# Splitting the eight PSUM banks two to six, not three to five, in the middle stage of a hybrid transformer layer

## Chip, cores and metric

The kernel runs on one core of a Trainium2 chip. The metric is the device time of one execution in microseconds (us). The core has five engines that run side by side: PE (matrix products, with weight loads listed apart as PEld), DVE, ACT and POOL (elementwise work) and SP (which issues transfers). Matrix products land in PSUM, which has eight banks of 128 x 512 fp32 values; another engine must read a result out of its bank ("evict" it) before the bank can hold the next one.

## The reference

One inference step of one layer, in fp32, on 256 prompt tokens and 8 decode tokens (one new token for each of 8 sequences). Model width 2048, FFN width 5504.

```python
x = x + 0.5 * swiglu(rmsnorm(x, n1), f1g, f1u, f1d)      # first FFN
h = rmsnorm(x, nm)
proj = h @ w_in                                           # 2048 x 4864
# columns of proj: q (1024), k, v (256 each), and the RWKV columns
o_att  = attend(q, k, v, sinks)        # window 128, 16 q heads, 4 kv heads
o_rwkv, shift, S = rwkv_time_mix(proj[..., ATT_COLS:], shift0, wkv0, ...)
x = x + concat([o_att, o_rwkv]) @ w_out                   # 2048 x 2048
x = x + 0.5 * swiglu(rmsnorm(x, n2), f2g, f2u, f2d)      # second FFN
y = rmsnorm(x, final_norm)
```

The RWKV-7 part mixes each token with its predecessor, and then runs, for each of 16 heads, a recurrence over a 64 x 64 state: `S = S*exp(logw) + (S @ -kk) * (kk*a) + v * k`, output `S @ r`. Outputs are y for both kinds of tokens, the new key and value caches, the RWKV states and the last projected columns.

## The kernel before

**Layout and precision.** Activations lie with features on the 128 partitions and the T = 264 tokens (256 + 8) along the free axis, so x is 16 tiles of 128 x 264. Each fp32 product is made of three: weights and activations are split into a rounded part (`hi`) and a rest (`lo`), and `gemm` (L143) issues hi·hi, hi·lo and lo·hi for each 128 x 128 weight block. The weights stream from memory in chunks of four blocks: `chunk` (L125) issues the transfer on SP into one of seven `raw` buffers, ACT casts `hi` (in the profile L136), and DVE subtracts for `lo` (L58), seven buffers each.

**Stages.** The first FFN (0 to about 706 us of the trace), the middle stage (to about 1133 us), and the second FFN. In each FFN the 43 blocks of the FFN width are handled in six parts; a part computes gate and up products, then 16 down products of eight or seven blocks (24 or 21 matmuls), each of which DVE adds to the residual from its bank (L297, recorded in the profile as L61). In the last part each such tile is also split and squared for the next norm (`nxt`), a square on ACT and a sum on POOL.

**The middle stage** (`mixing_body`) computes 38 input products of 48 matmuls each (`win(t)`, L411): two for the low-rank RWKV columns, 24 for r, k, v of eight head pairs, four for attention's k and v, eight for q. Its large products are evicted on DVE with high priority. The small work is written as generators: `prep` (a head pair's decay, keys and inner products), `chain` (a batch of two pairs: a triangular inverse by forward substitution on DVE with tiles `X`, `Xt`, `st`, then matrix products and the state passing), `attend` (one q tile of attention: scores, softmax, transposes, values), `kvtask`, `dec_load` and `dec_attend` (decode attention). After each weight chunk `tick` advances every live generator by one step, so small products are strewn among the large ones. Last comes the output projection, in three passes over 4, 6 and 6 of the 16 `mixed` tiles (`PASS`); each pass makes 16 products of 12 or 18 matmuls, adds them to the residual `xr`, and starts when the tiles it needs are mixed and split (`split`, L936; the cast is L939).

**Banks.** One pool `pp` holds all PSUM: tag `acc`, NACC = 3 banks, for large products, tag `m`, NM = 5 banks, for small ones and the first part of each FFN. `acc()` and `mp()` hand out the next bank of a kind, and whoever gets it waits until its last content has been read. In the middle stage a bank of kind `m` serves everything from the inner products of `prep` to transposes.

**Order.** A list scheduler with a cost model (not the order of the code alone) sets the order of instructions on each engine; within an engine they run in this order. Priorities, `keep_in_program_order` and `issue_after` bind it at places. In the profile all elementwise calls through helpers carry the helper's line: `tt` L58, `stt` L61, `act` L68, `mm` L74.

Of the kernel before, what the change touches and what calls it, by code (L numbers as in the profile page):

```python
# [7 lines left out]
F32 = mybir.dt.float32  # L8
# [5 lines left out]
P = 128  # L14
# [11 lines left out]
PARTS = [8, 7, 7, 7, 7, 7]  # L26
BATCH = [2, 2, 2, 2]
CH, NRAW, NHL = 4, 7, 7
NACC, NM = 3, 5
NS, NO, NY, NH, NT, NLD = 38, 8, 8, 40, 18, 6  # L30
NWARM = 7
NGM, NKR, NUV, NTT, NBT = 10, 5, 3, 2, 5
# [15 lines left out]
def body(tc, I, O):  # L48
# [4 lines left out]
    def uid(s):  # L53
        cnt[0] += 1
        return f"{s}{cnt[0]}"

    def tt(e, out, a, b, op):
        return e.tensor_tensor(out=out, in0=a, in1=b, op=op)  # L58
# [8 lines left out]
    def act(out, in_, f, **k):  # L67
        return A.activation(out=out, in_=in_, func=f, **k)  # L68
# [4 lines left out]
    def mm(out, lhsT, rhs, start=True, stop=True, **k):  # L73
        TE.matmul(out, lhsT, rhs, start=start, stop=stop, **k)  # L74
# [17 lines left out]
    def drain(only, hold=()):  # L92
        while any(g in only for g in tasks):
            tick(hold)
# [9 lines left out]
    with ExitStack() as ctx:  # L104
        cp = ctx.enter_context(tc.tile_pool(name="cp", bufs=1))
        sp = ctx.enter_context(tc.tile_pool(name="sp", bufs=1))
        wp = ctx.enter_context(tc.tile_pool(name="wp", bufs=1))
        pp = ctx.enter_context(tc.tile_pool(name="pp", bufs=1, space=bass.MemoryType.PSUM))
        dp = ctx.enter_context(tc.tile_pool(name="dp", bufs=1, space=bass.MemoryType.DRAM))
        cur = [None]  # L110

        def slot(shape=(P, T), dt=F32, tag="s"):
            return sp.tile(list(shape), dt, tag=tag, bufs={"s": NS, "o": NO, "y": NY}[tag], name=uid(tag))
# [3 lines left out]
            return pool.tile(list(shape), dt, tag="t", bufs=n, name=uid("t"))  # L117

        def acc():
            return pp.tile([P, 512], F32, tag="acc", bufs=NACC, name=uid("acc"))  # L120

        def mp():
            return pp.tile([P, 512], F32, tag="m", bufs=NM, name=uid("m"))

        def chunk(src, n, ahead=True):  # L125
            w = n * P
# [33 lines left out]
        ones = cp.tile([P, P], F32, name="ones")  # L160
# [3 lines left out]
        G.memset(eps[:, 1:2], 64e-5)  # L164
        act(eps[:, 0:1], eps[:, 0:1], AF.Copy)

        warm = mp()
        for _ in range(NWARM):
            mm(warm[:, :P], ones, ones)

        def vc(i):
            return vec[:, i:i + 1]
# [129 lines left out]
        def first_ffn(n2):  # L302
            xr = []

            def load(k0):
                n1.split(xr[k0], k0 > 1, e=None if k0 else V)

            def nxt(o):
                n2.split(xr[o])
                n2.square(xr[o])  # L310
                A.dma_start(xsp[o], xr[o])

            with tc.tile_pool(name="f1", bufs=1) as fp:
                cur[0] = (fp, NH)
                keep = tc.keep_in_program_order

                def weights(i):
                    raw = wp.tile([P, CH * P], F32, tag="raw", bufs=NRAW, name=uid("raw"))
                    keep(SP.dma_start(raw[:, :2 * P], I["gu1"][i // 2, i % 2][:, :2 * P]))
                    pre.append(raw)  # L320

                def inputs(n):
                    xg = fp.tile([P, n, T], F32, name=f"xg{len(xr)}")
                    k = KD + len(xr) * T
                    keep(SP.dma_start(xg.rearrange("p k t -> p (k t)"), I["xT"][:, k:k + n * T]))
                    xr.extend(xg[:, j] for j in range(n))

                def begin(k0, i):
                    n = {(2, 0): 2, (2, 2): 2, (4, 1): 2, (4, 3): 2, (8, 1): 2, (8, 3): 2}.get((k0, i))
                    if n:  # L330
                        inputs(n)

                x0 = fp.tile([P, T + KD], F32, name="x0")
                keep(SP.dma_start(x0, I["xT"][:, :T + KD]))
                n1 = Norm(VG1, gain=x0[:, T:])
                xr.append(x0[:, :T])
                for i, n in enumerate((1, 0, 0, 0, 0, 2)):
                    weights(i)
                    if n:
                        inputs(n)  # L340
                ffn(n1, xr, I["gu1"], I["dn1"], nxt, load, begin)
# [30 lines left out]
        def mixing(n2, n3, XD):  # L372
            with tc.tile_pool(name="mx", bufs=1) as mx:
                cur[0] = (mx, NT)
                return mixing_body(mx, n2, n3, XD)

        def mixing_body(mx, n2, n3, XD):
# [33 lines left out]
            def win(t):  # L411
                ps = acc()
                gemm(ps, I["win"][t], n2.xs, tick)
                if not have[0]:
                    n2.rstd(rs)
                    have[0] = True
                return ps
# [478 lines left out]
            for kind, i in SEQ:  # L896
# [10 lines left out]
                elif kind == "kv":  # L907
                    w, p = i // 2, i % 2
                    ps = win(LKV + i)
# [6 lines left out]
                else:  # L916
                    ps = win(LKV + 4 + i)
# [14 lines left out]
            xr = [slot() for _ in range(KD)]  # L932
# [3 lines left out]
            def split(i):  # L936
                hi, lo = slot(dt=F32R), slot(dt=F32R)
                m = pairs(mixed[i])
                A.copy(halves(hi), m)  # L939
                tt(V, halves(lo), m, halves(hi).bitcast(F32), ALU.subtract)  # L940
                mixed[i] = (hi, lo)

            def need(ks):
                return [bat[k // 2] for k in ks if k < 8] + [g for k in ks if k > 7 for g in att[k - 8]]

            k0 = 0
            for pi, ks in enumerate(PASS):
                now = need(ks)
                drain(now, [g for g in tasks if g not in now])
                with tc.high_priority():  # L950
                    for k in ks:
                        split(k)
                for o in range(KD):
                    ps = acc()
                    gemm(ps, I["wout"][o, :, k0 * P:(k0 + len(ks)) * P], [mixed[k] for k in ks], tick)
                    with tc.high_priority():
                        tt(V, xr[o], ps[:, :T], xr[o], ALU.add)
                    if pi == len(PASS) - 1 and o < CH:
                        n3.split(xr[o], tag="y")
                for k in ks:  # L960
                    mixed[k] = None
                k0 += len(ks)
            return xr

        def second_ffn(n3, xr, XD):
            fin = Norm(VGF, 3)

            def load(k):
                if k >= CH:
                    n3.split(xr[k], True, "o" if k in NSO else "s")  # L970

            with tc.tile_pool(name="f2", bufs=1) as fp:
                cur[0] = (fp, NH)
                ys = [fp.tile([P, 4, T], F32, tag="y", bufs=4, name=uid("y")) for _ in range(4)]
                rt = fp.tile([88, 8], F32, name="rt")

                def nxt(o):
                    fin.square(xr[o])
                    if o == 0:
                        act(rt[:, 7:8], fin.sums[0][0][0:88, 0:1], AF.Sqrt)  # L980
                    act(ys[o // 4][:, o % 4], xr[o], AF.Copy, scale=vc(VGF + o))

                side = dec_state(fp, XD)
                ffn(n3, xr, I["gu2"], I["dn2"], nxt, load, False, side)
                assert next(side, side) is side
                p = fin.sums[0]
                sm, rp, rq, hot = (mp() for _ in range(4))
                for i, q in enumerate(p):
                    for j in range(3):
                        mm(sm[0:88, j:j + 1], q[:, j * 88:j * 88 + 88], ones[:, 0:1], i + j == 0, i > 0,  # L990
                           skip_group_check=True)
                for _ in range(4):
                    mm(hot[:, :P], ones, p[1][:, :P])
                act(rt[:, 0:3], sm[0:88, 0:3], AF.Sqrt, scale=1.0 / D, bias=eps[0:88, 0:1])
                V.reciprocal(rt[:, 0:3], rt[:, 0:3])
                for r in (rp, rq):
                    for j in range(3):
                        mm(r[:, j * 88:j * 88 + 88], bc(rt[:, j:j + 1], (88, P)), C[0:88, CID:CID + 88])
                rs = fp.tile([P, T], F32, name="rs")
                A.copy(rs, rq[:, :T])  # L1000
                for i, (o, n) in enumerate(((0, 1), (1, 1), (2, 2), (12, 1), (4, 4), (13, 1), (8, 2), (14, 1), (10, 2), (15, 1))):
                    y = ys[o // 4][:, o % 4:o % 4 + n]
                    e, r = (V, rp[:, :T]) if o < 12 else (G, rs)
                    tt(e, y, y, bc(r.unsqueeze(1), (P, n, T)), ALU.mult)
                    (SP, A)[i % 2].dma_start(O["yT"][:, o:o + n, :], y)

        xsp = [dp.tile([P, T], F32, tag=f"xsp{o}", name=f"xsp{o}") for o in range(KD)]
        n2, n3 = Norm(VGM), Norm(VG2)
        first_ffn(n2)
        with tc.tile_pool(name="dx", bufs=1) as dx:  # L1010
            XD = dx.tile([P, 8, NPAIR, NB], F32, name="XD")
            second_ffn(n3, mixing(n2, n3, XD), XD)


OUTS = dict(yT=(P, KD, T), kp=(2, P, P), vp=(2, P, P), ks=(NB, P, 256), vs=(NB, P, 256),
# [99 lines left out]
```

## Time and profile before

| | us |
|---|---|
| median of three runs (lowest, highest) | 1848.77 (1846.81, 1850.28) |
| profiled execution | 1846.21 |
| its span | 1844.4 |
| PE busy in the span | 1821.4 |
| middle stage, 706 to 1133 us: length | 427.0 |
| middle stage: PE busy | 415.9 |
| middle stage: DVE busy | 349.3 |
| middle stage: ACT busy | 307.3 |

In rows of single instructions the first number is the start in us, the second the duration, then engine, line, operation, output and inputs, and in square brackets the time that the engine stood idle just before and what ended it. Durations of matmuls overlap, since they are pipelined; the step from one start to the next is what each costs. In rows of stretches the clock is the share of full speed that PE was granted. Tile names are without numbers: `acc` and `m` are banks, `s`, `t`, `o`, `y` activation tiles, `xg` the residual of the first FFN.

### The profile page before, as it was taken

The page shows a single profiled execution, that of the slowest core. Times are in us where ns is not written, and L with a number is a line of the kernel's source. Part 1 is how long each engine was busy: PE and PEld are TensorE (multiplying, and loading weights), DVE is VectorE, ACT ScalarE, POOL GpSimd, SP SyncE. Part 2 cuts the span into 40 slices and gives each one's busy share as a digit, 9 for nine tenths or more (in the row PEclk, how much of TensorE's full clock was granted, in tenths as well). Part 3 has the DMA queues.
Part 4 walks back from the last instruction along what each step waited for, and adds up shares of the span by engine and source line. Part 5 has one row for each costly group of instructions (what it writes and reads, how often), then busy time and mean ns, then how long its engine had stood idle before and what let it go on. Part 6 is the DMA issues. An engine that isn't in the chain of part 4 may idle for free.

```text
span 1844.4 us, 46192 instructions
## 1 busy us (share of the span) xinstructions
PE 1821.4 (99%) x17212; PEld 1792.4 (97%) x17212; DVE 1311.4 (71%) x2613; ACT 1068.6 (58%) x2134; POOL 258.4 (14%) x389
## 2 busy tenths in 40 slices
PE   9999999999999999999998999999999999999998
PEld 9999999999999999998987899999999999999997
DVE  6966665656656577799888677876766676667765
ACT  6645555455554557777767766654545555455555
POOL 0401101010010122122111200220101001010012
PEclk9999999999999999999999999999999999999999
DMA  8666666666666677555666446666666666666664
GB/s 270 191 202 213 196 210 205 201 199 188 204 190 201 196 201 244 174 169 146 174 174 183 143 127 220 185 201 189 203 207 208 193 211 203 203 208 193 216 189 136
DMA packets 226465, 358.25 MB, mean 194 GB/s; under 512 B 38440, under 2 KB 82112, under 8 KB 226240
## 3 DMA queue, kind: packets, MB, share of 16 engines
q1 hardware_dynamic: 220352, 349.20, 62.9%
q10 hardware_dynamic: 5888, 6.11, 1.1%
q8 instruction: 135, 2.21, 0.5%
q14 instruction: 90, 0.74, 0.1%
HBM read 347.06 MB, written 10.22 MB: 194 GB/s over the span
## 4 chain that ended last, share of the span: by engine, by line
PE 91%; DVE 3%; DMA 3%; issue 1%; ACT 1%; POOL 0%; SPq 0%; POOLq 0%; ACTq 0%; DVEq 0%
PE acc L74 84%; PE m L74 6%; DVE lo L58 1%; DMA raw<-in_gu 1%; DMA raw<-in_win 0%; DVE Xt L58 0%; DVE st L58 0%; DMA X<-sa 0%; ACT hi L136 0%; DMA sa<-gm 0%; DMA out_vp<-s 0%; DVE t L61 0%; DMA s<-xsp 0%; DVE t L459 0%; DMA ld<-in_bias 0%
## 5 line engine op out<-in xcount | busy, mean ns | idle before, releaser
L58 DVE TENSOR_TENSOR lo<-raw,hi 128x512 fp32r<-128x512 f32 (+2 forms) x1312 | 876.5, 673 | 443.9 <-ACT hi L136 417.2
L136 ACT CAST hi<-raw 128x512 fp32r<-128x512 f32 (+2 forms) x1312 | 774.9, 596 | 665.0 <-PE acc L74 438.8
L74 PE MATMUL acc<-s,hi 128*128 128x264 f32 x5940 | 1030.6, 278 | 2.7 <-ACT s L939 1.2
L74 PEld LDWEIGHTS acc<-s,hi 128*128 128x128 f32 x5940 | 899.3, 189 | 9.4 <-ACT hi L136 2.2
L74 PE MATMUL acc<-s,lo 128*128 128x264 f32 x2970 | 824.2, 278 | 0.0
L74 PEld LDWEIGHTS acc<-s,lo 128*128 128x128 f32 x2970 | 561.8, 189 | 2.3 <-issue 0.9
L74 PE MATMUL acc<-t,hi 128*128 128x264 f32 x2752 | 465.0, 276 | 0.0
L74 PEld LDWEIGHTS acc<-t,hi 128*128 128x128 f32 x2752 | 414.9, 189 | 0.0
L74 PE MATMUL acc<-t,lo 128*128 128x264 f32 x1376 | 379.2, 276 | 0.0
L58 POOL TENSOR_TENSOR t<-t,t 128x264 f32<-128x264 f32 (+1 forms) x148 | 145.3, 981 | 1063.6 <-ACT hi L136 986.0
L74 PEld LDWEIGHTS acc<-t,lo 128*128 128x128 f32 x1376 | 260.1, 189 | 0.0
L74 PE MATMUL acc<-y,hi 128*128 128x264 f32 x648 | 113.8, 277 | 0.0
L74 PEld LDWEIGHTS acc<-y,hi 128*128 128x128 f32 x648 | 97.8, 189 | 0.2
L74 PE MATMUL acc<-y,lo 128*128 128x264 f32 x324 | 89.4, 276 | 0.0
L58 DVE TENSOR_TENSOR t<-acc,t 128x264 f32<-128x264 f32 x156 | 67.2, 431 | 20.6 <-PE acc L74 12.0
L58 POOL TENSOR_TENSOR o<-o,o 128x264 f32<-128x264 f32 x43 | 35.7, 829 | 195.8 <-ACT o L68 189.0
L74 PEld LDWEIGHTS acc<-y,lo 128*128 128x128 f32 x324 | 61.2, 189 | 0.0
L74 PE MATMUL acc<-o,hi 128*128 128x264 f32 x324 | 58.8, 276 | 0.0
L74 PEld LDWEIGHTS acc<-o,hi 128*128 128x128 f32 x324 | 48.8, 189 | 0.0
L61 DVE SCALAR_TENSOR_TENSOR s<-acc,s 128x264 f32<-128x264 f32 x96 | 40.9, 430 | 8.8 <-PE acc L74 6.3
L289 ACT CAST t<-t 128x264 fp32r<-128x264 f32 x86 | 38.3, 445 | 13.6 <-POOL t L58 8.1
L74 PE MATMUL m<-s,hi 128*128 128x264 f32 x260 | 44.8, 277 | 0.6 <-ACT hi L136 0.6
(246 smaller groups left out, 1266.5 us busy)
## 6 DMA issues: line engine op xcount, KB each, us to landing
raw<-in_gu SPq DMA_DIRECT2D x680, 256.0 KB, 3.4
raw<-in_dn SPq DMA_DIRECT2D x224, 256.0 KB, 3.0
raw<-in_win SPq DMA_DIRECT2D x152, 256.0 KB, 3.7
raw<-in_dn SPq DMA_DIRECT2D x160, 192.0 KB, 2.7
raw<-in_wout SPq DMA_DIRECT2D x48, 256.0 KB, 3.3
raw<-in_wout SPq DMA_DIRECT2D x32, 128.0 KB, 2.8
s<-xsp SPq DMA_DIRECT2D x16, 132.0 KB, 3.5
raw<-in_gu SPq DMA_DIRECT2D x16, 128.0 KB, 3.9
```

The lines of the kernel that those rows point to most:

```text
L58: return e.tensor_tensor(out=out, in0=a, in1=b, op=op)
L61: return V.scalar_tensor_tensor(out=out, in0=a, scalar=s, in1=b, op0=op0, op1=op1)
L74: TE.matmul(out, lhsT, rhs, start=start, stop=stop, **k)
L136: A.copy(hi[:, :w], raw[:, :w])
L289: A.copy(halves(hi), pairs(u))
```

## The change

The single pool becomes three that follow each other: `pa` for the warm-up products and the first FFN, `pb` for the middle stage, `pc` for the second FFN. The first and third have three `acc` and five `m` banks as before, the middle one two and six (`NPB` = 2). In the output projection odd products take a bank of kind `m`, even ones of kind `acc`.

```diff
-NACC, NM = 3, 5
+NACC, NM, NPB = 3, 5, 2
...
-        pp = ctx.enter_context(tc.tile_pool(name="pp", bufs=1, space=bass.MemoryType.PSUM))
...
+        @contextmanager
+        def banks_of(name, *n):
+            with tc.tile_pool(name=name, bufs=1, space=bass.MemoryType.PSUM) as pool:
+                bank[0] = (pool, *n)
+                yield
...
         def acc():
-            return pp.tile([P, 512], F32, tag="acc", bufs=NACC, name=uid("acc"))
+            pool, n, _ = bank[0]
+            return pool.tile([P, 512], F32, tag="acc", bufs=n, name=uid("acc"))
...
         def mp():
-            return pp.tile([P, 512], F32, tag="m", bufs=NM, name=uid("m"))
+            pool, _, n = bank[0]
+            return pool.tile([P, 512], F32, tag="m", bufs=n, name=uid("m"))
...
-        warm = mp()
-        for _ in range(NWARM):
-            mm(warm[:, :P], ones, ones)
+        def warm():
+            w = mp()
+            for _ in range(NWARM):
+                mm(w[:, :P], ones, ones)
...
-                    ps = acc()
+                    ps = mp() if o % 2 else acc()
                     gemm(ps, I["wout"][o, :, k0 * P:(k0 + len(ks)) * P], [mixed[k] for k in ks], tick)
...
-        first_ffn(n2)
+        with banks_of("pa", NACC, NM):
+            warm()
+            first_ffn(n2)
         with tc.tile_pool(name="dx", bufs=1) as dx:
             XD = dx.tile([P, 8, NPAIR, NB], F32, name="XD")
-            second_ffn(n3, mixing(n2, n3, XD), XD)
+            with banks_of("pb", NPB, NACC + NM - NPB):
+                xr = mixing(n2, n3, XD)
+            with banks_of("pc", NACC, NM):
+                second_ffn(n3, xr, XD)
```

Each engine gets the same instructions, but for two ACT table loads fewer; the order differs from somewhat behind the start of the middle stage to its end, and is the same in both FFNs. At the borders of the pools the first product that takes a bank of the new pool waits until the old pool's last contents have been read: the first projection product for DVE's eviction of the last down product (before, for that of two products earlier), and the first gate product of the second FFN for the eviction of the last output product.

DVE, in the middle stage: the steps `st` and `Xt` are the forward substitution of the last batch, `kr<-m` and `N<-m` are evictions of small products of the batch before it. Before:

```order
L58 TENSOR_TENSOR Xt_14789<-Xt_14789,st_15492 128x5x11
L58 TENSOR_TENSOR st_15543<-X_14788,Xt_14789 128x60
L58 TENSOR_TENSOR Xt_14789<-Xt_14789,st_15543 128x6x10
L58 TENSOR_TENSOR st_15546<-X_14788,Xt_14789 128x54
L58 TENSOR_TENSOR Xt_14789<-Xt_14789,st_15546 128x6x9
L58 TENSOR_TENSOR kr_12776<-m_15223,kr_12776 128x192
L58 TENSOR_TENSOR kr_13282<-m_15223,kr_13282 128x192
L58 TENSOR_TENSOR st_15597<-X_14788,Xt_14789 128x48
L58 TENSOR_TENSOR Xt_14789<-Xt_14789,st_15597 128x6x8
L58 TENSOR_TENSOR st_15600<-X_14788,Xt_14789 128x42
L58 TENSOR_TENSOR N_15161<-m_15252,wc 128x512
```

The same place of the changed kernel:

```order
L58 TENSOR_TENSOR Xt_14793<-Xt_14793,st_15496 128x5x11
L58 TENSOR_TENSOR st_15547<-X_14792,Xt_14793 128x60
L58 TENSOR_TENSOR kr_12780<-m_15227,kr_12780 128x192
L58 TENSOR_TENSOR kr_13286<-m_15227,kr_13286 128x192
L58 TENSOR_TENSOR Xt_14793<-Xt_14793,st_15547 128x6x10
L58 TENSOR_TENSOR st_15550<-X_14792,Xt_14793 128x54
L58 TENSOR_TENSOR Xt_14793<-Xt_14793,st_15550 128x6x9
L58 TENSOR_TENSOR N_15165<-m_15256,wc 128x512
```

The two `kr` evictions moved three substitution steps earlier, and `N` three steps as well.

PE, in attention: the four products into one bank (`m_15904` before, `m_15908` now) are the values product of one q tile, each of them behind a transposed softmax tile `t`; `acc` rows are matmuls of large products. Before:

```order
L74 MATMUL m_15851<-uv_15730,bk_15732 32x128 x8
L74 MATMUL m_15851<-s_14402,bk_15732 32x1 x8
L74 MATMUL m_15904<-t_15745,s_14845 64x256
L74 MATMUL acc_16188<-s_10600,lo_16334 128x264
L74 MATMUL m_15904<-t_15809,s_14845 64x256
L74 MATMUL m_15904<-t_15746,s_14845 64x128
L74 MATMUL acc_16421<-s_16405,hi_16423 128x264
L74 MATMUL acc_16489<-s_16405,hi_16491 128x264
L74 MATMUL acc_16604<-s_16405,hi_16606 128x264
L74 MATMUL m_15904<-t_15810,s_14845 64x128
```

The same place of the changed kernel:

```order
L74 MATMUL m_15855<-uv_15734,bk_15736 32x128 x8
L74 MATMUL m_15855<-s_14406,bk_15736 32x1 x8
L74 MATMUL m_15908<-t_15749,s_14849 64x256
L74 MATMUL acc_16053<-s_9998,lo_16056 128x264
L74 MATMUL acc_16053<-s_10041,hi_16055 128x264
L74 MATMUL acc_16053<-s_10042,hi_16055 128x264
L74 MATMUL acc_16053<-s_10041,lo_16056 128x264
L74 MATMUL acc_16053<-s_10084,hi_16055 128x264
L74 MATMUL acc_16053<-s_10085,hi_16055 128x264
L74 MATMUL m_15908<-t_15813,s_14849 64x256
L74 MATMUL m_15908<-t_15750,s_14849 64x128
```

Before, one matmul of the last projection product stands between the first two values products, and three matmuls of three begun output products follow; now six matmuls of a projection product stand there, and the output projection begins later.

More of the change, by code (lines that the diff above doesn't have):

```diff
@@ L1 @@
 import math
-from contextlib import ExitStack, nullcontext
+from contextlib import ExitStack, contextmanager, nullcontext
 import numpy as np
@@ L107, in body @@
         wp = ctx.enter_context(tc.tile_pool(name="wp", bufs=1))
-        pp = ctx.enter_context(tc.tile_pool(name="pp", bufs=1, space=bass.MemoryType.PSUM))
         dp = ctx.enter_context(tc.tile_pool(name="dp", bufs=1, space=bass.MemoryType.DRAM))
-        cur = [None]
+        cur, bank = [None], [None]
+        @contextmanager
[3 more added lines that the diff above has]
+                yield
         def slot(shape=(P, T), dt=F32, tag="s"):
```

## The prediction

> **What bounds the kernel now.** I read the page's shares first, then the span cut at the two stage borders, then what TensorE (PE) waits for in the middle stage, then single stretches in time order.
>
> ```profile
> PE 1821.4 (99%) x17212; PEld 1792.4 (97%) x17212; DVE 1311.4 (71%) x2613; ACT 1068.6 (58%) x2134; POOL 258.4 (14%) x389
> 0.00:706.00 706.00, 703.13 (x6214) 701.46 (x6215) 470.08 (x792) 383.77 (x695) 91.93 (x101) 1.00 0.68 205
> 706.00:1133.00 427.00, 415.88 (x4753) 389.34 (x4752) 349.28 (x978) 307.32 (x762) 75.97 (x190) 1.00 0.59 171
> 1133.00:1844.40 711.40, 702.38 (x6250) 701.62 (x6248) 492.03 (x845) 377.49 (x680) 90.47 (x99) 1.00 0.65 197
> ```
>
> The columns of the last three rows are the stretch, its length, busy time of PE, weight load, DVE, ACT and POOL, PE's clock and the DMA share. PE is the bound throughout. The change keeps the matmuls, so it can move only what PE does not use: in the middle stage 427.00 − 415.88 = 11.1 us. DVE is 349/427 = 82% busy there, so evictions, which run on DVE, come late. This is what PE waits for in 700 to 1140 us (total, times, longest):
>
> ```profile
> PE m L74 <- DVE Xt L58: 3.2, 3, 1.6
> PE m L74 <- DVE st L58: 2.0, 1, 2.0
> PE acc L74 <- ACT s L939: 1.2, 1, 1.2
> PE m L74 <- DVE mxv L796: 1.0, 1, 1.0
> PE m L74 <- ACT t L809: 1.0, 1, 1.0
> PE m L74 <- ACT t L68: 0.8, 1, 0.8
> PE m L805 <- DVE t L810: 0.5, 1, 0.5
> PE m L74 <- DVE gm L58: 0.5, 2, 0.3
> ...
> PE m L74 <- POOL o L58: 0.2, 1, 0.2
> ```
>
> With two small waits left out (0.2 each) they sum to 10.8 us, nearly all of it at small products. That is the most that the sixth small bank can bring, besides a clock dip priced below.
>
> **1. The border from the first FFN to the middle stage: +3.7 us.** The changed kernel closes one set of PSUM banks and opens another. In the built program the first projection product now waits for the eviction of the last down product; before it waited for the eviction two products earlier. How late that eviction is, DVE and PE rows tell:
>
> ```profile
> 706.81 0.42 DVE L61 SCALAR_TENSOR_TENSOR xg<-acc,xg 128x264 f32<-128x264 f32 x1
> 709.49 0.42 DVE L61 SCALAR_TENSOR_TENSOR xg<-acc,xg 128x264 f32<-128x264 f32 x1
> 705.51 0.28 PE L74 MATMUL acc<-t,lo 128*128 128x264 f32 x1
> 705.63 0.39 PE L74 MATMUL acc<-s,hi 128*128 128x264 f32 x2
> 710.69 0.76 PE L74 MATMUL acc<-s,hi 128*128 128x264 f32 x2
> 711.74 0.49 PE L74 MATMUL m<-o,ones 128*128 128x264 f32 x1 [0.18 <-POOL o L58]
> 712.00:846.00 134.00, 134.00 (x1354) 1.00 0.64 190
> ```
>
> The first two rows are DVE's last two evictions of down products, 2.68 us apart. PE starts a matmul each 0.11 us (705.51 to 705.63), so the 21 matmuls of a down product of seven blocks take about 2.4 us: DVE has fallen behind. PE goes straight from the last down product (705.51) to the projection (705.63), but the last eviction ends at 709.49 + 0.42 = 709.91. So PE would stand from 705.6 to 709.9, about 4.3 us. Of this some 0.6 us exists already: the pair at 710.69 lasts 0.76 instead of 0.39, and 0.18 is waited at 711.74, both for the end of the same chain of squares, which does not move. Net +3.7; bounds 3.0 (DVE catches up a little while PE stands) and 4.3. Nothing gives it back: in the next 134.00 us PE is busy for 134.00. The third projection product needs the first one's bank already (two banks, not three); a product takes 48 × 0.11 = 5.3 us, so two give an eviction over 5 us, and I cost this at nothing; its cover gone, it would be what the chain of squares and the norm add after 711.74, bounded by the 2.7 us DVE period.
>
> **2. The border to the second FFN: +1.1 us.** The same holds there, with the last output product.
>
> ```profile
> 1133.02 0.39 PE L74 MATMUL acc<-y,hi 128*128 128x264 f32 x2
> 1133.08 0.69 DVE L58 TENSOR_TENSOR lo<-raw,hi 128x512 fp32r<-128x512 f32 x1
> 1133.69 0.42 DVE L58 TENSOR_TENSOR s<-acc,s 128x264 f32<-128x264 f32 x1
> ```
>
> PE would start not at 1133.02 but after 1133.69 + 0.42 = 1134.11. Bounds 0.4 (the weight split of 0.69 us ahead of it, at 1133.08, runs later) and 1.5.
>
> **3. The clock: +0.1 us.** The rows give stretch, length, PE busy (records), granted clock.
>
> ```profile
> 973.33:976.74 3.41, 1.79 (x49) 1.00 0.28 74
> 1007.44:1010.86 3.42, 2.41 (x45) 1.00 0.79 218
> 1010.86:1014.27 3.41, 2.27 (x12) 1.00 0.93 274
> 1014.27:1017.68 3.41, 3.33 (x15) 0.50 0.99 339
> ```
>
> Once in the stage the clock fell to 0.50 for 3.41 us, behind a poorly filled stretch, and cost half of that, 1.7 us. The stretch at 973 us was filled worse and did not do it, so it isn't a matter of the share alone. If step 5 closes the holes at 1010 us, I take 0.8 of this dip as gone (−1.4). The hole of 4.3 us in step 1 is longer than any here, and I give it a dip of its own at 0.9 of 1.7 (+1.5). Bounds −1.7 (old gone, none new) and +1.7 (old stays, one new).
>
> The Trainium skill's "TensorE: Matmul & The Clock Gate" (section "HAM oscillation — how this bites in real kernels") states that idle gaps over about 3.4 us put the clock to half, which speaks against this change. By that rule the new dip is sure and the sum below would be 0.2 us higher; without any new dip it would be 1.5 us lower. The trace holds no gap of that length, so no row decides it; the old dip came with single gaps of 1.0 us, so gap length alone doesn't describe this case.
>
> **4. RWKV chain beside attention, at 977 us: −2.4 us.**
>
> ```profile
> 977.14 0.92 PE L74 MATMUL m<-s,o 64*128 64x256 f32 x8 [2.02 <-DVE st L58]
> 979.78 0.33 PE L805 MATMUL m<-C,t 128*128 128x128 f32 x1 [0.54 <-DVE t L810]
> 976.38 0.62 DVE L58 TENSOR_TENSOR kr<-m,kr 128x192 f32<-128x192 f32 x2
> 977.50 0.69 DVE L58 TENSOR_TENSOR N<-m,wc 128x512 f32<-128x512 f32 x1
> ```
>
> The score product `m<-s,o` waits for a small bank: the one that `kr<-m` empties, whose end is 976.38 + 0.62 = 977.00. DVE runs `kr` among the steps of the fourth chain (`st`, `Xt`). With a sixth bank the scores need not wait for it, and in the new order `kr` also stands three steps earlier and `N` directly behind it. So 2.02 goes; of the 0.18 (for `N`) and 0.54 behind it I leave 0.3. Bounds −2.7 (all) and 0 (the next product then waits for the same `kr` and `N`).
>
> **5. Scores and decode at 1010 us: −2.0 us.**
>
> ```profile
> 1010.34 0.65 PE L74 MATMUL m<-t,s 128*64 128x256 f32 x2 [1.01 <-DVE mxv L796]
> 1012.27 0.65 PE L74 MATMUL m<-t,s 128*64 128x256 f32 x4 [0.98 <-ACT t L809]
> ```
>
> Between the four value products PE has one large matmul, then three; in the new order there are six between the first two and many more afterwards, since the last projections are not yet done. 1.99 us of waits are covered by 6 × 0.11 = 0.7 us and what follows; as the small products also come earlier relative to their inputs, I take all of it as gone, with bounds −2.0 and −0.7.
>
> **6. The last pass of the output projection: −1.4 us.**
>
> ```profile
> 1102.07 0.85 PE L74 MATMUL acc<-s,hi 128*128 128x264 f32 x4 [1.17 <-ACT s L939]
> ```
>
> The last decode transpose releases the splits (L939) that pass 3 needs, and PE waited 1.17 us with three products begun and interleaved; that interleaving also splits the chunks' use. In the new order the transpose stands some nine products ahead of pass 3, 9 × 18 × 0.11 = 18 us. The wait goes and about 0.2 us of broken pairs; bounds −1.4 and −1.0.
>
> **7. New waits of two large banks: +2.4 us.** No row of before shows them. (a) The sixth q product waits in the built program for the eviction of the product two before it, as only two banks hold large products. That eviction is in DVE's row of `st` and `Xt`; bounds 0 and the 2.0 of the longest such wait; I take 0.7. (b) The output projection alternates banks, and in its first pass PE takes the products out of turn: odd ones are held back while small tasks own the banks, so weight chunks are consumed in another order than they are made, from seven buffers.
>
> ```profile
> L58 DVE TENSOR_TENSOR lo<-raw,hi 128x512 fp32r<-128x512 f32 (+1 forms) x234 | 150.6, 653 | 37.2 <-ACT hi L136 33.7 <-PE acc L74 0.9
> 1015.00:1107.00 92.00, 90.68 (x998) 0.99 0.45 134
> ```
>
> A chunk costs DVE 0.65 us, and feeds 12 matmuls = 1.3 us. I count five chunks in the new order that are wanted less than one chunk's time after their buffer comes free. Half a `lo` each gives 5 × 0.33 = 1.7; bounds 0 and 5 × 0.65 = 3.3. Before, this stretch lost only 92.00 − 90.68 = 1.3 us, which includes the 1.17 of step 6.
>
> The waits of the earlier projection (0.8 for ACT, the 3.2 for `Xt`, the longest at 930 us) hang on data, not on a bank, and stay. ACT loses two table loads; ACT is 307/427 busy and doesn't bind: nothing.
>
> **Sum.** 3.7 + 1.1 + 0.1 − 2.4 − 2.0 − 1.4 + 0.7 + 1.7 = +1.5 us. The profiled execution took 1846.21 (span 1844.4), the median of three is 1848.77, 2.6 above it and within their spread. I add the sum to the median: 1850.3, forecast 1850. About 0.2%, 3.7 us, can be told from no change: faster is below 1845.1, slower above 1852.5.
>
> **The rivals.**
> - *Faster:* the three clusters 4 to 6 go fully with the old dip, no dip comes at the border, and step 7 comes to nothing. 3.7 + 1.1 − 1.7 − 2.7 − 2.0 − 1.4 = −3.0, and if the `Xt` waits shrink by half, −4.6: 1844. For it: every such wait is at a small product. Against: DVE's 82%.
> - *Slower, the bank is not what is missing:* DVE is. The eviction order on DVE decides, the same waits move to the next instruction, steps 4 and 5 bring half or less (−2.0 instead of −4.4), the old dip stays: 1.5 + 2.4 + 1.4 = +5.3, 1854. It decides from the point at which the scores at 977 us still wait over 1 us. For it: `st` and `Xt` rows around `kr`. Against: the new DVE order.
> - *The clock:* a hole of this length halves the clock for sure, over two stretches of 3.41 us and not one, and the old dip stays because holes of 1 us remain around it. 1.5 − 1.5 + 2 × 1.7 + 1.4 = +4.8: 1853 to 1854. It decides once the hole reaches a whole stretch. For it: the dip at 1014 us. Against: 973 us. The skill's page named in step 3 supports its first half.
> - *Weight chunks:* the first output pass loses a whole `lo` at each of ten chunks, 6.5 in place of 1.7: 1.5 + 4.8 = +6.3, 1855. Against: DMA moves only 134 GB/s there (the last number of the 1015 us row), so the raw chunks are early.
> - *The borders cost nothing:* DVE's last evictions come earlier than in the rows above, and no dip follows: 1.5 − 4.8 − 1.5 = −4.8, 1844. Against: on DVE nothing ahead of those two evictions has moved.
>
> **How the numbers follow.** Forecast 0.42; faster 0.24 and free borders 0.01; slower by DVE 0.14, by the clock 0.11, by the chunks 0.08. So faster by over 0.2% is 0.25, within 0.42, slower 0.33. The bounds of the steps added up give −4.2 (1844.6) and +11.1 (1860); all the high ends together are not likely. Low end 1843, the faster case with 1 us more; high end 1856, the chunk case with 1 us more. The forecast's own range is 1846 to 1852.
>
> **What would show it.** After: a PE hole of 3.5 to 4.3 us behind the last down matmul, released by DVE `xg`; the next stretch of 3.4 us at 0.50 clock; a hole near 1 us before the second FFN; `m<-s,o` at about 977 us without a wait over 0.5; no 1.17 for L939; clock 1.00 around 1015 to 1020. Wrong if PE's hole at the border is under 2 us, if stage waits for small products stay at 8 us or more, or if the first output pass loses over 4 us.

## The result: 13 us slower, outside the forecast range

The changed kernel takes 1861.26 us (median of four runs, 1859.3 to 1863.34), the kernel before, run beside it, 1847.85. The ratio is 1.0072, with a 95% interval of 1.006 to 1.0084. The forecast was 1850, with 1843 to 1856 as its range.

The profiled execution of the changed kernel has a span of 1858.5 us. Its shares, and the same three stretches as before, the second border taken where the second FFN now starts:

```profile
PE 1830.5 (98%) x17212; PEld 1801.5 (97%) x17212; DVE 1315.4 (71%) x2613; ACT 1068.5 (57%) x2132; POOL 257.2 (14%) x389
0.00:706.00 706.00, 703.40 (x6210) 701.67 (x6210) 471.63 (x793) 384.03 (x695) 91.71 (x101) 1.00 0.69 206
706.00:1146.70 440.70, 424.09 (x4755) 397.63 (x4755) 353.14 (x980) 308.32 (x761) 75.23 (x189) 0.98 0.58 166
1146.70:1858.50 711.80, 703.02 (x6248) 702.19 (x6248) 490.60 (x842) 376.16 (x677) 90.29 (x99) 0.99 0.66 196
```

The second FFN is as long as before (711.8 and 711.4 us), and the first is no longer (its last matmul starts at 704.5, before at 705.5). The middle stage grew from 427.0 to 440.7 us. Two numbers of that row matter: PE is busy 8.2 us longer (424.1, before 415.9) with the same matmuls, at a mean clock of 0.98, and idle 5.5 us longer. What PE waited for in the stage (total, times, longest):

```profile
PE acc L74 <- DVE xg L61: 4.3, 1, 4.3
PE acc L74 <- DVE o L61: 2.8, 1, 2.8
PE m L74 <- DVE st L58: 2.6, 3, 1.9
PE acc L74 <- DVE lo L58: 2.2, 2, 1.9
PE m L74 <- DVE Xt L58: 2.0, 2, 1.2
PE acc L74 <- DVE s L58: 1.4, 2, 1.1
PE m L74 <- DVE gm L58: 0.8, 1, 0.8
PE m L74 <- ACT t L68: 0.7, 1, 0.7
PE m L814 <- POOL t L65: 0.5, 1, 0.5
```

They sum to 17.3 us (with 1.1 at the second border), against 10.8. Four of the nine groups are large products (`acc`) that wait for DVE; before there was no such group. The rest of the loss is the clock. Stretches of 3.41 us, each pair the one ahead of a dip and the dip (length, PE busy, granted clock):

```profile
705.53:708.94 3.41, 0.00 (x0) 1.00 0.83 270
708.94:712.35 3.41, 3.29 (x15) 0.50 0.79 250
869.36:872.77 3.41, 2.23 (x56) 1.00 0.23 66
872.77:876.18 3.41, 3.36 (x34) 0.50 0.37 94
876.18:879.60 3.42, 3.42 (x18) 0.50 0.44 109
934.21:937.62 3.41, 1.46 (x26) 1.00 0.80 250
937.62:941.04 3.42, 3.42 (x18) 0.50 0.17 33
958.10:961.52 3.42, 1.08 (x10) 1.00 0.69 175
961.52:964.93 3.41, 2.93 (x13) 0.50 0.33 105
1077.57:1080.98 3.41, 1.47 (x10) 1.00 0.40 115
1080.98:1084.39 3.41, 3.41 (x18) 0.50 0.59 139
```

Six stretches ran at half clock, before one. All begin at a multiple of 3.413 us from each other, so there is a fixed grid. The ledger of the two profiled executions, whose spans are 14.1 us apart: PE is busy for 19.8 us in the six half-clock stretches, and for 3.3 in the one before; half of the difference, 8.2 us, is what the clock cost, the same 8.2 by which PE is busy longer. The 5.5 us of idle time make most of the rest (the waits listed are 6.5 us more).

### The profile page after: what moved, and what is told of

The parts are those of the page before. It is cut to its first block, busy times and chain, and to the rows that moved or that the text cites. A ratio compares the mean times of both kernels' runs of the same rounds, so it can differ in the third digit from the quotient of the medians.

```text
span 1858.5 us, 46186 instructions
## 1 busy us (share of the span) xinstructions
PE 1830.5 (98%) x17212; PEld 1801.5 (97%) x17212; DVE 1315.4 (71%) x2613; ACT 1068.5 (57%) x2132; POOL 257.2 (14%) x389
## 4 chain that ended last, share of the span: by engine, by line
PE 93%; DVE 3%; DMA 1%; ACT 1%; issue 1%; POOL 0%; SPq 0%; POOLq 0%; ACTq 0%; DVEq 0%
PE acc L74 84%; PE m L74 9%; DVE lo L58 1%; DMA raw<-in_gu 1%; ACT hi L143 0%; DVE st L58 0%; DVE Xt L58 0%; ACT t L68 0%; DMA sa<-gm 0%; PE m L548 0%; DVE t L467 0%; DMA raw<-in_win 0%; DVE t L61 0%; ACT L68 0%; DMA bk<-vnd 0%
## 5 line engine op out<-in xcount | busy, mean ns | idle before, releaser
L74 PE MATMUL acc<-s,hi 128*128 128x264 f32 x5684 | 993.7, 279 | 7.9 <-DVE xg L61 4.3
L74 PEld LDWEIGHTS acc<-s,hi 128*128 128x128 f32 x5684 | 866.2, 190 | 13.7 <-ACT hi L143 6.1
L74 PE MATMUL acc<-s,lo 128*128 128x264 f32 x2842 | 791.5, 279 | 2.4 <-DVE lo L58 2.4
L74 PEld LDWEIGHTS acc<-s,lo 128*128 128x128 f32 x2842 | 540.9, 190 | 4.8 <-DVE lo L58 3.0
L74 PE MATMUL m<-s,hi 128*128 128x264 f32 x516 | 90.7, 279 | 0.0
L74 PEld LDWEIGHTS m<-s,hi 128*128 128x128 f32 x516 | 78.2, 190 | 0.9 <-issue 0.5
L74 PE MATMUL m<-s,lo 128*128 128x264 f32 x258 | 71.0, 277 | 0.0
```

## The experiments

Theory 1 says that PE's holes cost their length and, where they leave a stretch thin, half of the next. The rivals are that the split alone, or the borders alone, or DVE's lateness is the cause. "Before" was timed again beside every group of runs, and each ratio is to it.

| run | pools; large/small banks in the middle stage; odd output products | median us | ratio to before (95%) |
|---|---|---|---|
| changed kernel | 3; 2/6; small | 1861.3 | 1.0072 (1.0060 to 1.0084) |
| e1 | 3; 3/5; large | 1856.3 | 1.0049 (1.0036 to 1.0063) |
| e2 | 1; 2/6; small | 1862.9 | 1.0084 (1.0071 to 1.0098) |
| e3 | 1; 2/6, output 3/5; large | 1857.6 | 1.0057 (1.0045 to 1.0070) |
| e4 | 1; 3/5; small | 1855.8 | 1.0047 (1.0034 to 1.0059) |
| f1 | changed, first hole filled | 1858.9 | 1.0064 (1.0051 to 1.0077) |
| f2 | e1, first hole filled | 1850.2 | 1.0015 (1.0007 to 1.0024) |
| f3 | 3; 2/6; large | 1855.5 | 1.0046 (1.0031 to 1.0061) |
| f4 | changed, every other q product small | 1868.1 | 1.0112 (1.0098 to 1.0126) |
| g1 | changed, Vt apart | 1863.4 | 1.0080 (1.0064 to 1.0096) |
| g2 | f1 + f3 + g1 | 1858.2 | 1.0055 (1.0042 to 1.0068) |
| g3 | 1; third bank lent late, Vt apart | 1852.1 | 1.0025 (1.0016 to 1.0035) |
| g4 | before, Vt apart | 1844.1 | 0.9978 (0.9969 to 0.9987) |
| h1, h2 | f2, fill with 1/4, 1/2 of the array | 1850.9, 1850.5 | 1.0022 (1.0013 to 1.0031), 1.0018 (1.0009 to 1.0027) |
| h3 | f2, fill with 1/16 of the array | 1852.7 | 1.0028 (1.0018 to 1.0039) |

**The borders alone.**

```diff
-NACC, NM, NPB = 3, 5, 2
+NACC, NM, NPB = 3, 5, 3
-                    ps = mp() if o % 2 else acc()
+                    ps = acc()
```

> Three pools in sequence, but three large and five small banks in each and no alternation: the borders alone, with the order of before. Theory 1 (holes of PE plus the half-clock stretches they set off; the first border is one of several): the hole of 4.3 us behind the last down product and its dip, 4.3 us in all by the shift of later products in the changed kernel, plus 1.1 at the second border: 5.4 us slower than before, 1853. Rival A (the split of the banks alone makes the loss, the borders are hidden): 0 to 1 us slower. Rival B (the borders are everything, since a shifted start moves all dips): 10 us or more slower.

Measured: 9.3 us slower than before (1856.29 against 1846.96), so 4 us more than theory 1 expected, and near rival B. The instruction order is that of before but for a few dozen rows. The stretches at the first border:

```profile
705.00:708.06 3.06, 0.00 (x0) 1.00 0.80 251
708.06:711.47 3.41, 2.20 (x10) 0.50 0.75 249
711.47:714.88 3.41, 3.41 (x17) 0.50 0.46 160
```

The hole of 4.3 us brought two half-clock stretches, not one, and two more came at 875 and 984.5 us, in clusters of small products whose waits are those of before (1.06 and 2.01 us; before 1.06 and 2.02). What differs is their place on the grid.

**The split and the alternation without borders, and each alone.** One pool, from which a third large bank is lent:

```diff
+        def acc():
+            turn[0] += 1
+            if not lent[0] and turn[0] % 3 == 0:
+                return pp.tile([P, 512], F32, tag="x", bufs=1, name=uid("acc"))
+            return pp.tile([P, 512], F32, tag="acc", bufs=2, name=uid("acc"))
...
+            if lent[0] and turn[1] % 6 == 0:
+                return pp.tile([P, 512], F32, tag="x", bufs=1, name=uid("m"))
+            return pp.tile([P, 512], F32, tag="m", bufs=5, name=uid("m"))
```

> One pool for the whole kernel; one of the eight banks is lent from the large to the small products in the middle stage, so two to six there, with alternation in the output projection, and no border. Theory 1: 13.4 less the 5.4 of the borders, about 8 us slower than before (1856): the waits for a bank at the q products (2.8) and for weight chunks in the output projection (1.9) stay, each with a half-clock stretch of 1.7. Rival A: the whole 13 us stay. Rival B: within 2 us of before.

> As the version with the lent bank, but the bank goes back to the large products before the output projection, and those take large banks only, as before. Theory 1: the q wait of 2.8 and its dip of 1.7 stay, the chunk wait of 1.9 and its dip go: 4 to 5 us slower than before (1852). Rival (the alternation is harmless or useful): as slow as the version with alternation, about 8 us.

> The kernel before with one edit: odd output products take a small bank; one pool, three large and five small banks. Theory 1: the waits for chunks come with the alternation (up to 2 us and a dip of 1.7), against which the 1.2 us before the last pass may go: 1 to 3 us slower. Rival (chunks come out of turn only because the sixth bank reorders the small tasks): no change, within 1 us, or 1 us faster.

All three came out slower than theory 1 had them: 15.9, 10.7 and 8.8 us over before. The parts don't add. Without the border's hole the split shows a wait that the hole had covered, that of the third projection product for the first one's bank (2.33 us in e2, whose row this is, 2.51 in e3).

```profile
719.25 0.46 PE L74 MATMUL acc<-s,hi 128*128 128x264 f32 x2 [2.33 <-DVE pj L58]
```

Holes and clock are not all of it, either. In the profiles of e2, e3 and g3 below, the three kernels with a lent bank, PE's busy time less half of what lies in half-clock stretches is 1824.5 to 1825.0 us, against 1819.7 before and 1819.9 in the changed kernel: some 5 us that no wait shows, and whose cause stays open.

The alternation alone costs more than its late chunks. The four longest of what PE waited for in e4 from 1016 to 1110 us, where before there is a single wait of 1.2 us:

```profile
PE acc L74 <- DVE lo L58: 2.1, 3, 1.2
PE m L805 <- ACT t L777: 2.1, 2, 1.5
PE m L74 <- ACT t L809: 1.2, 1, 1.2
PE m L74 <- ACT TT L639: 1.0, 1, 1.0
```

The chunks (`lo`) come as forecast, but the small products of attention and of the last chain, now later in relation to the large ones, wait more, and two half-clock stretches follow there from 1041 us on.

**The hole filled.** 36 products that nobody reads, on a tile that is ready, right behind the last down product, in the changed kernel (f1) and in e1 (f2):

```diff
             first_ffn(n2)
+            w, h = mp(), n2.xs[13][0]
+            for _ in range(NFILL):
+                mm(w[:, :T], h[:, :P], h)
```

> The changed kernel with 36 idle products (264 columns, on a tile that is ready, into a spare small bank; 36 x 0.11 = 4.0 us) behind the last down product: PE works through the hole, nothing else is changed. Theory 1 (a hole costs its length, and half of each 3.41 us stretch that it puts to half clock): the hole's length stays, its half-clock stretch goes: 1.7 us (one stretch) to 3.4 us (two) faster than the changed kernel, 1858 to 1859.5. Rival (the clock costs nothing there, since the next products have slack): as the changed kernel, 1861.

> The three-pool kernel with 3 and 5 banks in each (borders only), with the same 36 idle products in the first border's hole. Theory 1: its two half-clock stretches at the border go, 3.4 us faster than borders only: 1853. What is left over before is then the two holes, 4.3 - 0.6 + 1.1 = 4.8, and what later stretches add. Rival (clock costs nothing): 1856.

In e1 the fill takes 6.1 us off (1856.3 to 1850.2), more than expected. The hole keeps its length, so I read these two thirds of what the borders cost as clock; the mean granted clocks of the runs agree (0.9934 in e1, 0.9964 in f2, 0.9962 before). The fill and the stretch behind it run at full clock:

```profile
705.05:709.55 4.50, 4.49 (x38) 1.00 0.83 259
709.60:713.00 3.40, 3.40 (x30) 1.00 0.70 235
```

In the changed kernel it takes off 2.4 us between the medians, but 1.4 when each is set against the before of its own group (13.4 and 12.0 over), and the intervals of the ratios overlap (1.0060 to 1.0084, 1.0051 to 1.0077): at the low end of the expected 1.7 to 3.4, and not shown by itself.

**Without the alternation, and with one more.** The changed kernel with large banks for all output products (f3):

```diff
-                    ps = mp() if o % 2 else acc()
+                    ps = acc()
```

and, as f4, in `win`:

```diff
-                ps = acc()
+                ps = mp() if t >= LKV + 4 and t % 2 else acc()
```

> The changed kernel, with all output products in the two large banks. Theory 1 (the alternation lets products run out of turn, so weight chunks come late): the chunk waits of 2.2 us and a stretch of 1.7 go: 3.5 us faster than the changed kernel, 1857.5. Rival (two large banks are too few for products of 12 matmuls, 1.3 us): sixteen short waits for evictions in the first pass, 2 us or more slower than the changed kernel, 1863.

> The changed kernel, in which every other q product takes a small bank, so that none waits for the product two before it. Theory 1: the wait of 2.8 us and its stretch of 1.7 go: 4.5 us faster than the changed kernel, 1857. Rival (the DVE is late, so that the wait moves to the small products that lose the bank): within 1 us of the changed kernel.

f3 is 8.6 us over the before of its group, where the changed kernel is 13.4 over its own: 4.8 us faster (5.7 between the medians), so the rival (two banks too few for short products) falls. In its output projection the waits for `lo` are gone, and evictions (`DVE s`) cost 0.8 us in all. Against e1, f3 has the split alone added and is no slower (8.6 and 9.3 over). Along this path the loss is: borders 9.3, split about 0, alternation 4.8. On the path without borders the split alone cost 10.7 and the alternation alone 8.8, so these are prices of a path, not of the parts.

f4 went the other way, 21.1 us over before, 7.7 more than the changed kernel. The q wait stayed (2.69 at 961.97): the q product with a small bank starts only behind it, at 965.24, so I take it that no small bank was free at 962 us either. New waits came at the softmax transposes (L813), which use small banks:

```profile
PE m L813 <- ACT t L785: 3.2, 2, 2.0
PE acc L74 <- DVE lo L58: 1.3, 2, 1.0
PE m L892 <- DVE t L61: 1.2, 1, 1.2
```

**What held the large bank.** The last key/value product waited 15 us for its eviction in the changed kernel (its last matmul starts about 947.5; the eviction is the last row here), which left one bank to the q products:

```profile
962.00 0.81 PE L74 MATMUL acc<-s,hi 128*128 128x264 f32 x2 [2.81 <-DVE o L61]
961.52 0.42 DVE L61 SCALAR_TENSOR_TENSOR o<-acc,rs 128x264 f32<-128x264 f32 x1
962.75 0.43 DVE L58 TENSOR_TENSOR s<-acc,rs 128x264 f32<-128x264 f32 x1
```

In before, e1 and the changed kernel its eviction came 2 to 3 us behind the ACT copy into the slot that the code had asked for just before it, `Vt` of the other pair (in the changed kernel the copy ends at 959.7). My reading is that slots of one tag are handed out in the order of the code. So `Vt` got tiles of its own, with 36 slots in place of 38 (g1), the same in before (g4), with all fixes in three pools (g2), and in one pool with the bank lent from the second batch to the output projection only (g3):

```diff
-                    Vt[p] = slot((P, 2, P))
+                    Vt[p] = fix((P, 2, P), f"Vt{p}")
```

> The changed kernel, in which the transposed values of attention (Vt) have tiles of their own and no slot of tag s (38 slots become 36). In all builds so far the eviction of the last key/value product stands directly behind the copy into the Vt slot that was asked for before it, because slots of one tag are handed out in the order of the code; in the changed kernel its matmuls end at 947.5 and it is evicted at 962.8, so that one of the two large banks is blocked for 15 us. Theory 1: with that gone, the eviction comes within some us, the 2.8 us wait of the next q product and its half-clock stretch of 1.7 go: 4.5 us faster than the changed kernel, 1857. Rival (DVE is late anyway): the wait stays, 1861.

> The changed kernel with three edits together: 36 idle products in the first border's hole, all output products in the large banks, and Vt in tiles of its own. Three pools, two and six banks in the middle stage stay. Theory 1: 1861.3 less 2.4 (filled border), 4.8 (no alternation) and 4.5 (Vt) gives 1849.6, 2.7 us above before, which the holes at the two borders (4.3 - 0.6 + 1.1 = 4.8) more than explain. Rival (two large banks cost something throughout the stage): 1854 or more.

> One pool, no border; the third large bank is lent to the small products from the end of the first batch of projections to the start of the output projection only; no alternation; Vt in tiles of its own. Theory 1 (borders, the third projection product, the q wait and the alternation are the costs): all are gone, so within 2 us of before, and up to 4 us faster if the sixth bank shortens the waits at 977 and 1010 us. Rival (every new order of the middle stage meets new waits and half-clock stretches): 4 us or more slower than before.

> The kernel before with Vt in tiles of its own, nothing else. Theory 1 (a third large bank covers the blocked one): no wait was there, so within 2 us of before. Rival (the blocked bank costs before as well): 2 us or more faster. Rival (a new order meets new waits): 3 us or more slower.

In g1 the mechanism is shown and the gain is not. The eviction comes 16 us earlier, and the wait of 2.81 is gone:

```profile
946.88 0.42 DVE L58 TENSOR_TENSOR s<-acc,rs 128x264 f32<-128x264 f32 x1
957.78 0.42 DVE L61 SCALAR_TENSOR_TENSOR o<-acc,rs 128x264 f32<-128x264 f32 x1
967.11 0.43 DVE L61 SCALAR_TENSOR_TENSOR o<-acc,rs 128x264 f32<-128x264 f32 x1
```

But all that follows has a new order with waits of 1.76 (1002 us) and 1.91 (1077 us), and the time stays (the intervals of the ratios overlap). Its six runs price the clock: the same program took 1856.9 us at a mean clock of 0.996 and 1866.0 at 0.990. 0.006 of 1858 us is 11 us of clock, and it cost 9.1. g2 and g3 fell to the rival, 11 and 5 us over before: in g2 the border's fill still takes its 4.0 us, and both meet new thin clusters (four and three half-clock stretches in their profiles; g3 has a new wait of 2.69 for POOL at 842 us).

g4 was expected to change nothing and is the best kernel of the study: 1844.1, a ratio of 0.9978 (0.9969 to 0.9987). Its waits in the stage sum to 11.2 us, no less than the 10.8 of before, so the rival's reason (the blocked bank costs before as well) isn't what made it faster. In its profile no stretch runs at half clock until the last products are done. The clocks of all its runs point the same way: 0.9974 in the mean of nine, 0.9962 in the 18 of before, 2.3 us less lost, and the gain is 2.8. No run tests it further.

**What sets off half clock.** The matmul records from 700 to 1140 us of fifteen traces (all but those of g4, which has no dip in the stage, and of h3) were put on the grid of their execution, each in the stretch where it starts. Each stretch got its share: columns streamed x 0.417 ns (products of 264 columns start 0.11 us apart; the plain fp32 products `m<-t,C` of 264 columns start 0.22 us apart and count twice) x the share of rows and columns of the array in use, over 3413 ns. Of 1863 stretches at full clock, 46 lie below a share of 0.34, and 42 of these are followed by half clock; of the 1817 above, 4 are. PE's busy time separates worse (24 wrong at its best threshold, against 8). g4 fits: no stretch of it lies below 0.34. The fill puts this to the test: PE is busy for 4.0 us with a quarter (h1), half (h2) or a sixteenth (h3) of the array.

```diff
-                mm(w[:, :T], h[:, :P], h)
+                mm(w[:64, :T], h[:64, :64], h[:64])       # h1; h2: h[:, :64], h; h3: 32 for 64
```

> As the three-pool kernel with 3 and 5 banks and 36 idle products in the first border's hole, but each idle product uses a quarter of the array (64 of 128 rows, 64 of 128 columns) for the same 264 columns: PE is busy for the same 4.0 us. Theory 1 (the clock goes by the share of the array that works in a stretch of 3.41 us, and falls below about 0.35 to 0.45): the half-clock stretches at the border come back, as with borders only, 1855 to 1856. Rival (it goes by whether PE is busy at all): as with the full products, 1850.

> The same with idle products of half the array (128 rows, 64 columns). Theory 1: a share of 0.5, over the threshold, so no half-clock stretch at the border, 1850. Rival (columns and rows don't count alike, or the threshold lies higher): 1855 to 1856.

> As the quarter fill, with idle products of a sixteenth of the array (32 rows, 32 columns), PE busy for the same 4.0 us. With a quarter of the array a stretch falls below 0.34 only if 3.0 of its 3.41 us lie in the fill, which about 4 in 10 positions of the stretches allow, so that run could not tell the theories apart; with a sixteenth 2.4 us are enough, for about 9 in 10 positions, as with an empty hole. Theory 1 (share of the array): the half-clock stretch at the border is back, most runs as with borders only, 1855 to 1856. Rival (PE's busy time): 1850 to 1851, as the other fills.

h1 and h2 ran like the full fill. h1 missed its expectation, and in its profiled execution not for want of cover: the fill (from 705.09) takes up all but 0.2 us of a stretch, whose share is 0.22, and no half clock follows:

```profile
704.90:708.32 3.41, 3.41 (x30) 1.00 0.81 247
708.32:711.73 3.41, 3.36 (x29) 1.00 0.74 240
```

h3 missed its own in time too: 4.4 us over the before of its group (1848.28), where the full fill had 3.2, h1 4.1 and the empty hole 9.3. Its interval overlaps all of theirs (that of the empty hole only from 1.0036 to 1.0039). But its profile shows what busy time cannot explain, the fill, the stretch around its end and the next:

```profile
705.54 4.51 PE L75 MATMUL m<-s 32*32 32x264 f32 x36
707.37:710.79 3.42, 3.36 (x29) 1.00 0.81 263
710.79:714.20 3.41, 3.41 (x18) 0.50 0.58 189
```

PE is busy for 3.36 of 3.42 us, its share of the array is 0.23, and the next stretch has half clock. With h3's trace the count is 45 of 49 below the threshold and 5 of 1936 above. So busy time is ruled out as the measure, but so is rows times columns with one threshold, theory 1 of these runs: h1's 0.22 and h3's 0.23 are nearly the same share, with opposite outcomes. Counted by rows alone they are 0.44 and 0.36, on the two sides of that count's best threshold (0.415), yet it is wrong at 10 of the 1863 stretches (by columns alone 20, by neither 25). How rows and columns count is open. That h3 is not as slow as e1 can be read from the rows: its half-clock stretch is full of large products (3.41 of 3.41), and is the only one there, while in e1 the first one holds the end of the hole (2.20 of 3.41) and a second follows. That reading rests on one profile each and stays open too.

## Why the prediction was wrong

**The step that failed is 3, the clock:** forecast +0.1, measured five more half-clock stretches, 8.2 of the 14.1 us between the profiled spans. I priced one new dip and took the old one as chance, because the stretch at 973 us was emptier than the one that set it off. With the share of the array both agree: 973 us has 0.39 and no dip, 1010 us 0.29 and one. Holes of 1 to 3 us among small products stand at that edge all through the stage, and I had counted them by their length alone. The border's dip came and the old one went, as step 3 had them; five others came, from 873, 876, 938, 962 and 1081 us on, the third and the last of them behind these waits:

```profile
937.01 0.27 PE L74 MATMUL m<-N,PT 64*64 64x64 f32 x2 [1.95 <-DVE st L58]
1079.99 0.38 PE L74 MATMUL acc<-s,lo 128*128 128x264 f32 x1 [1.94 <-DVE lo L58]
```

The rule of the Trainium skill that I weighed there ("TensorE: Matmul & The Clock Gate", section "HAM oscillation — how this bites in real kernels", gaps over about 3.4 us) holds for the border's hole, but the dips from 938, 962 and 1081 us on followed gaps of 1.95, 2.81 and 1.94 us, so the gap's length alone does not decide here.

**Steps 1 and 2, the borders,** were right in the hole: 4.27 us released by `xg`, and 1.08 at the second. What hung on them, two stretches and the moved grid, was not; e1 gives 9.3 for the two, where steps 1 to 3 had 4.9 with the new dip at 1.5 and the old one off. What step 1 put at nothing, the third product's wait for the first one's bank, is 2.33 in e2 and 2.51 in e3, within the 2.7 it gave as the bound; in the changed kernel no such wait appears.

```profile
709.06 0.78 PE L74 MATMUL acc<-s,hi 128*128 128x264 f32 x2 [4.27 <-DVE xg L61]
1146.70 0.46 PE L74 MATMUL acc<-y,hi 128*128 128x264 f32 x2 [1.08 <-DVE s L58]
```

**Step 4** forecast −2.4; 2.74 us of waits became 1.17 (0.83 and 0.34), so −1.6: the scores still wait behind the chain's steps.

```profile
984.54 0.89 PE L74 MATMUL m<-s,o 64*128 64x256 f32 x6 [0.83 <-DVE Xt L58]
985.77 0.27 PE L74 MATMUL m<-N,PT 64*64 64x64 f32 x2 [0.34 <-DVE st L58]
```

**Step 5** was right: waits for `mxv` and for `t` of L809 are absent after (−2.0, of which 0.3 returns at a POOL wait). **Step 6** was right: the wait for L939 is absent (−1.2).

**Step 7a** was mis-sized, 0.7 against 2.81, and above its bound of 2.0: I had seen that the bank was held and not by what, nor for how long. The row of that eviction was in the trace of before, 21.6 us behind the start of its product's last matmul (935.20):

```profile
956.78 0.43 DVE L58 TENSOR_TENSOR s<-acc,rs 128x264 f32<-128x264 f32 x1
```

**Step 7b** forecast 1.7 and measured 2.5 (1.94 and 0.23 for `lo`, 0.30 for `s`), but the hole of 1.94 was also followed by a half-clock stretch, and the alternation as a whole cost 4.8 on top of f3.

By waits alone the forecast was +1.4 and the measured +6.5. Of the rivals, the clock one came nearest, at a price of 4.8 and a chance of 0.11, but its own particulars did not come: the border's hole brought one half-clock stretch in the changed kernel, and the old dip went. The rival of a late DVE did not come as it stood: the scores wait 0.83, under its 1 us, and steps 4 and 5 brought about 3.6 of their 4.4. The new waits are mostly for DVE all the same (`xg`, `o`, `lo`, `s`, 10.7 of the 17.3); at one of them g1 shows that the order on DVE, not a lack of time, held the bank. The low ends of the steps add up to −4.4 (1844.4), not −4.2; nothing hangs on it. The range failed, as I read it, because each row of small costs was bounded by itself, though all of them draw on the same thin stretches.

## What to carry to other kernels

A kernel that keeps PE 99% busy pays for its holes twice, once in length and once in the clock behind them. So count, for each stretch of the clock's grid, how much of the array works, and treat clusters of small products near a share of a third as places where any new wait can cost about 1.5 us more than itself. A new pool is a barrier: its first user waits for the last reader of the old one. The same split can be had in one pool by lending a bank, but here that was no faster (e2 is 15.9 us over before, the three pools 13.4). And a bank count says little by itself: look at how long each product's result stays in its bank, since one late eviction makes two banks into one.

## What the runs showed of the hardware, unexpected

The granted clock falls to 0.50 for whole stretches of 3.413 us on a fixed grid within an execution, in most cases after a stretch whose share of working array (rows x columns) is below about 0.34 (45 of 49, against 5 of 1936 above). The clearest exception is h1: a share of 0.22, on 64 x 64 tiles, with full clock behind it. PE's busy time in the profile doesn't tell it: a stretch with PE busy 98%, most of it on 32 x 32 tiles (h3), was followed by half clock.

One program took 1856.9 to 1866.0 us in six runs, with mean clocks from 0.996 to 0.990. The profiles have their grids at different places against the program, and in e1 the clusters of before meet half clock with the same waits. That the grid's place is what makes runs of one program differ is my reading; each program has one profile, so no pair of them shows it.
